# Second FFN product of an encoder step written as seven half-size block products

## The chip, the cores and the metric

The kernel runs on one core of a Trainium2 chip. The metric is the device time of one launch in microseconds (us), given as the median of the runs. The profile is of one execution and counts from the first to the last instruction of the program (its span). Engines: TensorE (PE) does matmuls and, beside them, weight loads (PEld); VectorE (DVE), ScalarE (ACT) and GpSimd (POOL) work element by element; SyncE (SP) issues nearly all DMAs.

## The reference, cut to what matters

One step of a two-layer encoder. Layer 0 is an SSD mixer and an FFN, layer 1 is band attention and an FFN. 1024 prompt frames and 64 sample frames go through the same weights, so the kernel treats them as 1088 columns.

```
D_MODEL = 1024; FFN_HIDDEN = 2816
def swiglu(u, w_in, w_out):
    g, up = jnp.split(u @ w_in, 2, axis=-1)
    return (jax.nn.silu(g) * up) @ w_out
...
x = x + post_norm(f(pre_norm(x)))      # every sub-layer, RMSNorm over D_MODEL
```

`u @ w_in` is called the first product here, `(...) @ w_out` the second. All is float32.

## The kernel before

**Layout and exactness.** Features lie on the 128 partitions, frames along the free axis. D_MODEL is 8 tiles (`KD`), the hidden width 22 tiles (`FT`). Each float32 operand is split into a rounded high part and a low rest; a product of one 128x128 weight tile takes three matmuls (high by high, high by low, low by high). The split costs one ACT cast and one DVE subtraction for weights (`Weights.part`, lines 342 and 343) and for activations alike. PE's order is the program's own order; the other engines' instructions are ordered by a scheduler with priorities. A virtual clock (`Stream`) decides where side tasks (generators with `yield`) put their instructions among the PE work.

**Frames.** Two partitions of the 1088 frames are in use: three slices `SL` of 384, 384 and 320, and four quarters `QS` of 256, 256, 288 and 288. Quarters 0 and 1 form block 0, quarters 2 and 3 block 1.

**First product.** It is already done by 2x2x2 blocks in seven products (`PRODS`: P1, P6, P2, P7, P5, P4, P3), with sums of weights made in `Weights.pair` (lines 290, 291, 308, 309) and sums of activations made once in `op_build`. `run_pair` computes one hidden tile for both blocks, 84 matmuls of 256 columns and 84 of 288, and evicts with DVE adds (lines 1328 to 1345); ACT applies silu and POOL multiplies gate by up (lines 1342, 1346). The first six hidden tiles are done in `plain_pairs` for block 0 alone, without the seven products; then 16 tiles for both blocks; then the first six for block 1. Each hidden tile is stored to DRAM (`hscr`, lines 1291, 1343, 1347).

**Second product.** In `back`, lines 1514 to 1516: for each of the three slices, for each of 8 output tiles, a sum over all 22 hidden tiles: 528 weight tiles x slice in all, three matmuls each. All weights are loaded and split once for each slice. `loader` (lines 1375 to 1377) reads hidden tiles back from DRAM, splits them and keeps a whole slice in SBUF. ACT evicts (line 1529), squares go to a running sum on POOL (line 493).

**After it.** `end` runs once for each slice: the root of the mean square (`rstd`, lines 500 to 524: PE transposes, ten small DVE operations), its broadcast (`bcast`, lines 530 and 533), scaling and residual add (lines 1430, 1431), store of x. In layer 0 it also splits the result into the operands of the attention layer (`u_slice`, `UC`: lines 1447, 1448) and makes the factor of the next norm, marked `("rb", s)`. Attention begins with K, V and Q projections of slices 0 and 1, which need `u[0]`, `u[1]`, and then the factor in their evictions; slice 2 follows. In layer 1 the last slice ends the kernel (lines 1404 to 1421).

**Buffers.** Big tiles come from two rings: `R` (16 tiles of 1152 columns) and `RX` (13 of 1024, per layer). `Ring.get` and `put` count tiles; a task waits in virtual time until a tile is free. Weights pass `raw` (2, and lent `RX` tiles) and `hl` (3 split tiles of 1024 columns).

Of the kernel before, what the change touches and what calls it, by code (L numbers as in the profile page):

```python
# [39 lines left out]
AT = mybir.DependencyInfo(mybir.DependencyClass.Sync, mybir.DependencyReason.DATA)  # L40

# [7 lines left out]
ES = 0.5, 0.5, 0.0  # L49
OS = 1.9, 1.4  # L50
EP_W, ER_W, EQ_W = (9.4, 9.4, 2.2), (8.9, 8.9, 3.3), (11.0, 11.0)
# [4 lines left out]
LDP, ENP, ATP = 1500, (0, 0, 1500), 1000  # L56
# [3 lines left out]
RAWB, HLB, SGB = 2, 3, 5  # L60
# [6 lines left out]
NACC = 3  # L67

# [155 lines left out]

class Weights:
# [44 lines left out]
    def plain(self, it):  # L270
        if not self.room():
            return False
        r, n = it["raw"][0], it.get("n", 1024)
        if it.get("kscale") is not None:
            self.scaled(it, r)
        else:
            self.part(it, "w", None, r[:, :n])
        it["of"][0].put()
        self.ready.append(self.sq.pop(0))
        return True  # L280
# [44 lines left out]
    def part(self, it, key, ring, v, eng=None, acc=None):  # L325
        if ring is not self.half:
            ring = self.hl if ring or self.hl.free() else self.hx
            self.used.append(ring)
# [50 lines left out]
def hybrid_kernel(  # L379
# [42 lines left out]
    hd_ = [dr.tile([P, FT, T], F32, name=f"hscr{i}") for i in range(2)]  # L422
# [9 lines left out]
    W.tc, W.lent = tc, Lent(RX)  # L432
    W.raws.append(W.lent)
    UC = Cells(384, (R, 99))

# [821 lines left out]

    def ffn_plan(layer):
        w1, w2 = w_f1[layer], w_f2[layer]
        W.plan(*[dict(src=[w1[i]], acc=t_ < NACC or t_ == NB0 - 1) for t_ in range(NB0) for i in (t_, FT + t_)])  # L1260
        for t_ in [*range(NB0, FT), *range(NB0)]:
            W.plan(dict(src=[w1[t_], w1[FT + t_]], pacc=t_ in (NB0, NB0 + 1)))
        for s in range(NSL):
            for m in range(KD):
                for k0, nk in KCH:
                    W.plan(dict(src=[w2[m][:, k0 * P:(k0 + nk) * P]], n=nk * P))

    KCH = ((0, 8), (8, 8), (16, 6))

    def plain_pairs(ts, ops, hd, px, tmp):  # L1270

        n = ops.n
        first = ts == PGS[0]
        xs, ws = {}, {}
        for t_, i, q in [(t_, i, q) for t_ in ts for i, q in (((0, 0), (1, 0), (0, 1), (1, 1)) if first else ((0, 0), (0, 1), (1, 0), (1, 1)))]:
# [4 lines left out]
            if i == 0:  # L1280
                xs[t_, q] = tmp.tile([P, n], F32, tag=("p1", "u3")[q] + f"{t_ % 2}", name="x")
# [6 lines left out]
            def mult(ps):  # L1288
                with tc.high_priority(HIP):
                    V.tensor_tensor(x, ps[:, :n], x, op=ALU.mult)  # L1290
                nc.sync.dma_start(hd[:, t_, q * n:(q + 1) * n], x)
# [5 lines left out]
    def run_pair(t_, pr, bs, ends, ops, hd, px, tmp, apart=False):  # L1297
# [3 lines left out]
        for (p_, key, c0, i), b in [(x, b) for b in bs for x in PRODS] if apart else [(x, b) for x in PRODS for b in bs]:  # L1301
# [3 lines left out]
            def t_new(tag):  # L1305
                return tmp.tile([P, n], F32, tag=f"{tag}{b if len(bs) > 1 else t_ % 2}", name=tag)
# [4 lines left out]
            for k in range(4):  # L1311
# [3 lines left out]
                PE.matmul(ps, wl, ah[:, k, :], start=False, stop=(k == 3))  # L1315
# [6 lines left out]
            with tc.high_priority(HIP):  # L1322
# [16 lines left out]
                elif p_ == P4:  # L1339
# [3 lines left out]
                    nc.sync.dma_start(hd[:, t_, BO[b] + n:BO[b] + 2 * n], x["u3"])  # L1343
                else:
                    V.tensor_tensor(x["u2"], ps, x["u2"], op=ALU.add)
                    G.tensor_tensor(x["c22"], x["p1"], x["u2"], op=ALU.mult)
                    nc.sync.dma_start(hd[:, t_, BO[b]:BO[b] + n], x["c22"])
# [6 lines left out]
    def back(layer, start, cpost, xsrc, xmid, cpre, cpost2, xout, rb_out, done2):  # L1354

        hd = hd_[layer]
        dn, ops, phase, hid = [], [Ops(0, layer), Ops(1, layer)], [0], [{}, {}, {}]
        with ExitStack() as es:
            px = pool(es, f"px{layer}", 4, space=PSUM)
            RX.pool, RX.bufs = pool(es, f"rx{layer}"), NRX  # L1360
            sgp = pool(es, f"sg{layer}")
            stage[0] = lambda: sgp.tile([P, 384], F32, tag="sg", bufs=SGB, name="sg")

            def loader():

                for s, (o, n) in enumerate(SL):
                    yield 0, 0, lambda: phase[0] > (s > 0)
                    cells = Cells(n, *(((RX, 99), (R, 8)), ((R, 9), (RX, 99)), ((RX, 99), (R, 3)))[s])
                    for k in range(FT):
                        yield 0, 0, lambda: cells.room(2)  # L1370
                        c = cells.get(), cells.get()
                        h_, l_ = rr(c[0][0]), rr(c[1][0])
                        t_ = stage[0]()[:, :n]
                        with tc.high_priority(LDP):
                            nc.sync.dma_start(t_, hd[:, k, o:o + n])
                            A.copy(h_, t_)
                            V.tensor_tensor(l_, t_, h_, op=ALU.subtract)
                        hid[s][k] = h_, l_, c, cells

            def end_load(s):  # L1380
                o, n = SL[s]
                xc = Cells(n, (R, 99)) if s == 2 else Cells(n, (RX, 99), (R, 99))
                yield 0, EP_W[s] if s < 2 else 0, lambda: xc.room(KD)
                xs = [xc.get() for _ in range(KD)]
                for m in range(KD):
                    nc.sync.dma_start(xs[m][0], xmid[:, m, o:o + n])
                xss[s] = xs, xc

            def end(s, y, ss, more=None):

                o, n = SL[s]
                if s not in xss:
                    yield from end_load(s)
                xs, xc = xss.pop(s)
                out = []
                if s == 2 and more is None:
                    yield 0, EP_W[2]
                steps = rb_steps(ss, n, out, ER_W[s], more=more)
                if more is not None:

                    xps = {}

                    def hold(ms):
                        for m in ms:
                            xps[m] = mm("xp") if m > 3 else px.tile([P, 512], F32, tag="mm", name="xp")
                            PE.matmul(xps[m][:, :n], ident, xs[m][0], start=True, stop=False)
# [6 lines left out]
                    for m in range(KD):  # L1413
                        ym = y[:, m, :n]
# [4 lines left out]
                        else:  # L1419
                            V.tensor_tensor(ym, ym, xs[m][0], op=ALU.add)  # L1420
                        nc.sync.dma_start(xout[:, m, o:o + n], ym)
                    for c in xs:
                        xc.put(c)
# [637 lines left out]
```

## Time and profile before

| | us |
|---|---|
| median of 3 runs | 2940.78 |
| lowest, highest | 2934.37, 2947.84 |
| profiled execution: span | 2929.9 |
| second product, layer 0 | 264.8 (from 1315.6 to 1580.4) |
| second product, layer 1 | 262.7 (from 2653.8 to 2916.5) |
| first product by pairs, layer 0 | 398.6 (from 917.0 to 1315.6) |

The profiled execution lies 10.9 us below the median of the runs and 4.5 us below the lowest of them, so a time worked out on the span is moved by the first of these to stand beside the median. Within the page: part 1 gives the busy time of each engine; matmuls overlap there, so their mean duration is not the distance from one to the next. That distance has to be read from starts in the timeline.

### The profile page before, as it was taken

The numbers are of one execution on the slowest core, as the hardware profiler recorded it, in microseconds if no ns is written. First come the engines' busy times: TensorE is split into PE (matmuls) and PEld (weight loads), VectorE is DVE, ScalarE is ACT, GpSimd is POOL, SyncE is SP. The second block draws the span as 40 slices with busy tenths as digits, with TensorE's granted clock in tenths as the row PEclk, the third lists the DMA queues.
The fourth block names the chain that finished last, engine by engine and source line by source line (L and its number), as shares of the span: only waits on it lengthen the run. The fifth ranks groups of instructions, "written<-read, shape, count | busy, mean of one in ns | idle before, by whom it ended". The sixth has DMA issues, their size and how long they took to land.

```text
span 2929.9 us, 56271 instructions
## 1 busy us (share of the span) xinstructions
PE 2897.3 (99%) x21562; PEld 2858.7 (98%) x21562; DVE 2027.6 (69%) x4452; ACT 1403.6 (48%) x2535; POOL 718.9 (25%) x884
## 2 busy tenths in 40 slices
PE   8999999999999999999999999999999999999999
PEld 8999999999999999999999899999999999999998
DVE  7988878885867555583567887778688554575544
ACT  6655546454544222353445665556664222244443
POOL 1333333331022434350111000000131434351111
PEclk9999999999999999999999999999999999999999
DMA  4423333335564222345664322223476222245654
GB/s 138 133 92 106 104 98 109 100 117 165 165 187 137 76 81 77 108 151 163 207 192 154 98 74 72 65 69 108 132 204 179 83 77 81 75 154 178 225 171 135
DMA packets 203422, 369.12 MB, mean 126 GB/s; under 512 B 20752, under 2 KB 149488, under 8 KB 203152
## 3 DMA queue, kind: packets, MB, share of 16 engines
q1 hardware_dynamic: 199920, 354.97, 38.3%
q0 software_dynamic: 3232, 10.56, 2.0%
q8 instruction: 169, 2.77, 0.4%
q14 instruction: 101, 0.83, 0.1%
HBM read 298.24 MB, written 62.74 MB: 123 GB/s over the span
## 4 chain that ended last, share of the span: by engine, by line
PE 88%; DVE 6%; DMA 2%; ACT 2%; issue 1%; SPq 0%; POOL 0%; DVEq 0%; ACTq 0%; POOLq 0%
PE px L1314 9%; PE px L1315 9%; PE px L1313 9%; PE mm L467 8%; PE mm L469 8%; PE mm L468 8%; PE po L1515 6%; PE po L1516 6%; PE po L1514 6%; PE mmx L468 3%; PE mmx L469 3%; PE mmx L467 3%; PE ptp L1747 2%; PE po L1782 2%; PE S L1716 1%
## 5 line engine op out<-in xcount | busy, mean ns | idle before, releaser
L467 PE MATMUL mm<-r,hl 128*128 128x384 f32 (+2 forms) x1704 | 566.6, 333 | 2.6 <-DVE vt L1679 1.0
L469 PE MATMUL mm<-r,hl 128*128 128x384 f32 (+2 forms) x1704 | 549.6, 323 | 1.0 <-DVE hl L343 0.7
L468 PE MATMUL mm<-r,hl 128*128 128x384 f32 (+2 forms) x1704 | 549.3, 322 | 0.0
L343 DVE TENSOR_TENSOR hl<-raw,hl 128x1024 fp32r<-128x1024 f32 x216 | 256.3, 1187 | 216.6 <-ACT hl L342 208.9
L1314 PE MATMUL px<-r,hl 128*128 128x288 f32 (+1 forms) x1184 | 347.6, 294 | 0.0
L467 PEld LDWEIGHTS mm<-r,hl 128*128 128x128 f32 x1704 | 321.9, 189 | 4.9 <-DVE vt L1679 1.3
L469 PEld LDWEIGHTS mm<-r,hl 128*128 128x128 f32 x1704 | 321.1, 188 | 1.9 <-DVE hl L343 1.0
L468 PEld LDWEIGHTS mm<-r,hl 128*128 128x128 f32 x1704 | 322.2, 189 | 0.3
L1315 PE MATMUL px<-r,hl 128*128 128x288 f32 x1056 | 311.5, 295 | 0.0
L1313 PE MATMUL px<-r,hl 128*128 128x288 f32 x1056 | 310.4, 294 | 0.0
L342 ACT CAST hl<-raw 128x1024 fp32r<-128x1024 f32 x216 | 216.8, 1004 | 162.5 <-PE po L1516 101.6
L493 POOL TENSOR_TENSOR ssum<-ssum,sq 128x256 f32<-128x256 f32 (+3 forms) x97 | 125.5, 1295 | 616.9 <-ACT sq L492 601.3
L1314 PEld LDWEIGHTS px<-r,hl 128*128 128x128 f32 x1184 | 222.4, 188 | 0.0
L1315 PE MATMUL px<-rx,hl 128*128 128x256 f32 x768 | 214.2, 279 | 3.6 <-DVE hl L343 3.5
L1313 PE MATMUL px<-rx,hl 128*128 128x256 f32 x768 | 213.9, 278 | 0.4 <-DVE x L1290 0.4
L1515 PE MATMUL po<-rx,hl 128*128 128x384 f32 (+1 forms) x624 | 202.0, 324 | 0.2
L1313 PEld LDWEIGHTS px<-r,hl 128*128 128x128 f32 x1056 | 198.9, 188 | 0.1
L1315 PEld LDWEIGHTS px<-r,hl 128*128 128x128 f32 x1056 | 198.9, 188 | 0.0
L1514 PE MATMUL po<-rx,hl 128*128 128x384 f32 (+1 forms) x608 | 197.7, 325 | 0.0
L1516 PE MATMUL po<-rx,hl 128*128 128x384 f32 (+1 forms) x608 | 196.7, 324 | 0.0
L1314 PE MATMUL px<-rx,hl 128*128 128x256 f32 x640 | 178.4, 279 | 0.0
L1514 PE MATMUL po<-r,hl 128*128 128x384 f32 (+1 forms) x448 | 148.4, 331 | 0.0
(367 smaller groups left out, 7890.1 us busy)
## 6 DMA issues: line engine op xcount, KB each, us to landing
raw<-in_w_f_dram SPq DMA_DIRECT2D x154, 512.0 KB, 3.7
rx<-in_w_f_dram SPq DMA_DIRECT2D x54, 512.0 KB, 3.7
raw<-in_w_in_dram SPq DMA_DIRECT2D x40, 512.0 KB, 3.7
MT<-ascr SPq DMA_DIRECT2D x48, 384.0 KB, 4.3
sg<-hscr SPq DMA_DIRECT2D x88, 192.0 KB, 3.4
raw<-in_w_f_dram SPq DMA_DIRECT2D x44, 384.0 KB, 3.2
raw<-in_w_so_dram SPq DMA_DIRECT2D x32, 512.0 KB, 3.7
raw<-in_w_o_dram SPq DMA_DIRECT2D x19, 512.0 KB, 3.6
```

The source lines that it names most:

```text
L342: self.nc.scalar.copy(h, v)
L343: (eng or self.eng or self.nc.vector).tensor_tensor(lo, v, h, op=ALU.subtract)
L467: PE.matmul(ps[:, :n], h_, xh, start=(first and i == 0), stop=False)
L468: PE.matmul(ps[:, :n], h_, xl, start=False, stop=False)
L469: PE.matmul(ps[:, :n], l_, xh, start=False, stop=(last and i == nk - 1))
L493: (eng or G).tensor_tensor(ssum[:, :n], ssum[:, :n], q[:, :n], op=ALU.add)
L1313: PE.matmul(ps, wh, ah[:, k, :], start=(k == 0), stop=False)
L1314: PE.matmul(ps, wh, al[:, k, :], start=False, stop=False)
L1315: PE.matmul(ps, wl, ah[:, k, :], start=False, stop=(k == 3))
L1514: PE.matmul(ps[:, :n], wh, xh, start=(k == 0), stop=False)
L1515: PE.matmul(ps[:, :n], wh, xl, start=False, stop=False)
L1516: PE.matmul(ps[:, :n], wl, xh, start=False, stop=(k == FT - 1))
```

## The change

**The second product by blocks.** The hidden axis is cut in halves (tiles 0 to 10 and 11 to 21, `KH` = 11), the output axis in halves (tiles 0 to 3 and 4 to 7), the frames of each block in its two quarters. Seven products follow, each of 4 output tiles x 11 hidden tiles x 2 blocks. Hidden tile pairs (k, k+11) are now computed one after the other, and their sums s1 to s4 are made by DVE at once (`hidden`), so that seven operands instead of the hidden tiles go to DRAM (`hc`). Four sums of the second weights are made by DVE during the first product of each layer and stored in DRAM (`w2_sums`). `loader` reads operands in groups of three or four tiles and splits them. `evict` adds up the products in place. Six products run for both blocks on one set of weights; the last, P4, runs for block 0 and then for block 1, and the weights of three of its four output tiles are kept in ring tiles (`Held`).

```
-for s, (o, n) in enumerate(SL):
-    for m in range(KD):
-        for k0, nk in KCH:            # ((0, 8), (8, 8), (16, 6))
+SEQ = tuple((p_, (0, 1)) for p_ in (P1, P6, P2, P5, P3, P7)) + ((P4, (0,)), (P4, (1,)))
+KCH, KHELD = ((0, 6), (6, 5)), ((0, 4), (4, 4), (8, 3))
+J4 = (0, 1, 2, 3), (1, 2, 3, 0)
+for x, (p_, bs) in enumerate(SEQ):
+    for j in J4[bs[-1]] if len(bs) == 1 else range(4):
+        for b in bs:
+            for c, (k0, nk) in enumerate(KHELD if keep else KCH):
+                for k in range(k0, k0 + nk):
+                    PE.matmul(ps[:, :n], wh, xh, start=(k == 0), stop=False)
+                    PE.matmul(ps[:, :n], wh, xl, start=False, stop=False)
+                    at_pe[0] = PE.matmul(ps[:, :n], wl, xh, start=False, stop=(k == KH - 1))
+            evict(p_, b, j, ps[:, :n])
```

Evictions, by DVE but for the first product (`add(t, x)` is one DVE add of the PSUM tile to x); P1 `A.copy(c11)`; P6 `add(c21, c11)`; P2 `add(c11, c11)`; P5 `add(c22, c21)`; P3 `add(c12, c22)`; P7 `add(c22, c22)` and `add(c21, c21)`; P4 `add(c21, c21)`. Quarters 0 and 2 are whole after P3, quarter 1 after P4 of block 0, quarter 3 after P4 of block 1; `ready` collects the squares and spawns `end`.

```
+def hidden(t_, b, x, z, late=None):       # x: first half of the block's frames, z: second
+    if not kh:
+        out(OPI["a11"], x)
+        out(OPI["s3"], total(s3, x, z, ALU.subtract))
+        kept[k, b] = z, s3
+        return
+    out(OPI["a12"], x)
+    out(OPI["a22"], z)
+    out(OPI["s1"], total(z0, z0, z, ALU.add))
+    s2 = total(stage[0]()[:, :n], z, s3, ALU.subtract)
+    out(OPI["s2"], s2)
+    out(OPI["s4"], total(stage[0]()[:, :n], x, s2, ALU.subtract))
...
+def w2_sums(layer, yet):                  # 16 times (4 tiles x 4 pieces of SUM_C = 352 columns)
+    paced(nc.sync.dma_start(t_, w2[m][:, a:a + SUM_C]))          # four loads
+    paced(V.tensor_tensor(b22, b22, b12, op=ALU.subtract))       # four DVE sums
+    paced(nc.sync.dma_start(wd[:, i, j, c:c + SUM_C], t_))       # four stores
...
+def loader():
+    yield 0, 0, lambda: phase[0] and stored.get((i, b)) == KH
+    yield 0, 0, lambda: any(r.free(2) for r in rings)
+    paced(nc.sync.dma_start(l_, hc[:, i, k:k + g, HO[b]:HO[b] + n]))
+def parted(p_, b, k, g, h_, l_, r):
+    paced(A.copy(rr(h_), l_))
+    paced(V.tensor_tensor(rr(l_), l_, rr(h_), op=ALU.subtract))
```

`paced` puts an instruction behind the last PE instruction in the scheduler's order and adds no wait on the chip. `hidden` stores 4.0 us (`HST`) of virtual time after the sums.

**Norms by quarter.** `end` runs for quarters. A slice of the attention operands needs two quarters: slice 0 needs 0 and 1, slice 1 needs 1 and 2, slice 2 needs 2 and 3; the same holds for the factors.

```
+EP_W, ER_W, EQ_W = (6.0, 5.0, 8.0, 4.0), (6.0, 4.0, 6.0, 4.0), (12.0, 14.0, 12.0, 16.0)
+SEG = (((0, 0, 256, 0),), ((0, 256, 384, 0), (1, 0, 128, 128)), ((1, 128, 384, 0),), ((2, 32, 320, 0),))
+for s, *_ in SEG[q]:
+    yield 0, 0, lambda: s in ucells or UC.room(2 * KD)
+...
+yield (0, EQ_W[q]) if q < 3 else (0, 0, lambda: "k2" in done2)
+yield from rb_steps(tot, n, [], ER_W[q], rb_out[:, o:o + n])
```

**Start of attention.** The matmuls of V and K for slice 0 are issued before the factor of slice 0 is there, then their evictions wait for it; Q of slice 0, then V, K and Q of slice 1 follow.

```
-for s in range(2):
-    st.wait_for(lambda: s in done)
-    for w, e in ((wv, evv), (wk, evk), (wq, evq)):
-        units(w, 0, e, (s,))
+st.wait_for(lambda: 0 in done)
+for w, e in ((wv, evv), (wk, evk)):
+    passes(ps, w, lambda k: u[0][k], [(k, k) for k in range(KD)], n0, parts=4)
+st.wait_for(lambda: ("rb", 0) in done)
+for ps, e in first:
+    e(0)(0, ps)
+units(wq, 0, evq, (0,))
+st.wait_for(lambda: 1 in done)
+for w, e in ((wv, evv), (wk, evk), (wq, evq)):
+    units(w, 0, e, (1,))
```

425 lines of the change are left out of this document (288 added, 137 removed).

## The prediction

> **What bounds the kernel now.** I read the page first: who is busy, at what clock, what chain ended last.
>
> ```profile
> span 2929.9 us, 56271 instructions
> ...
> PE 2897.3 (99%) x21562; PEld 2858.7 (98%) x21562; DVE 2027.6 (69%) x4452; ACT 1403.6 (48%) x2535; POOL 718.9 (25%) x884
> ...
> PEclk9999999999999999999999999999999999999999
> ...
> PE 88%; DVE 6%; DMA 2%; ACT 2%; issue 1%; SPq 0%; POOL 0%; DVEq 0%; ACTq 0%; POOLq 0%
> ```
>
> PE is busy almost throughout, at full granted clock. A busy PE may still be waiting inside its pipeline, so next come the windows, cut where the stages of the two FFNs begin and end (columns: PE, PEld, DVE, ACT, POOL, then clock, DMA share, GB/s).
>
> ```profile
> 833.40:917.00 83.60, 83.60 (x724) 83.60 (x723) 57.64 (x111) 39.02 (x55) 16.74 (x19) 1.00 0.79 220
> 917.00:1249.00 332.00, 329.78 (x2656) 329.41 (x2655) 181.67 (x317) 103.32 (x173) 125.18 (x109) 1.00 0.28 87
> 1249.00:1315.60 66.60, 66.60 (x506) 66.60 (x506) 54.09 (x84) 33.20 (x54) 35.19 (x28) 1.00 0.48 152
> 1315.60:1580.40 264.80, 264.59 (x1610) 263.87 (x1609) 144.91 (x219) 121.33 (x197) 37.06 (x28) 1.00 0.59 185
> ...
> 2653.80:2916.50 262.70, 262.70 (x1598) 262.56 (x1597) 121.88 (x165) 103.70 (x159) 31.81 (x24) 1.00 0.57 181
> 2916.50:2929.90 13.40, 8.73 (x41) 6.02 (x39) 6.54 (x20) 3.42 (x8) 0.00 (x0) 1.00 0.29 98
> ```
>
> The second product takes 264.8 and 262.7 us, and PE is idle for 0.2 us of it. Whether each pass runs at its own pace is read from starts in the timeline: 48 passes of 384 columns, 36 of 320, then runs of twelve of 256 and of 288 in the first product.
>
> ```profile
> 1399.79 0.33 PE L1516 MATMUL po<-rx,hl 128*128 128x384 f32 x1
> ...
> 1407.99 0.34 PE L1515 MATMUL po<-r,hl 128*128 128x384 f32 x1
> ```
> ```profile
> 1559.77 0.31 PE L1514 MATMUL po<-rx,hl 128*128 128x320 f32 x1
> ...
> 1564.90 0.31 PE L1516 MATMUL po<-rx,hl 128*128 128x320 f32 x1
> ```
> ```profile
> 1100.12 0.28 PE L1313 MATMUL px<-rx,half 128*128 128x256 f32 x1
> ...
> 1101.48 0.29 PE L1313 MATMUL px<-r,half 128*128 128x288 f32 x1
> ...
> 1103.07 0.28 PE L1313 MATMUL px<-rx,hl 128*128 128x256 f32 x1
> ...
> 1104.48 0.30 PE L1313 MATMUL px<-r,hl 128*128 128x288 f32 x1
> ...
> 1106.08 0.28 PE L1313 MATMUL px<-rx,hl 128*128 128x256 f32 x1
> ```
>
> 384 columns: 8.20 us over 47 steps, 0.1745 us. 320: 5.13 over 35, 0.1466. 256: 1.36 and 1.41 us for twelve, 0.1154. 288: 1.59 and 1.60, 0.1329. With these the old second product should take 352 x 3 x 0.1745 + 176 x 3 x 0.1466 = 261.7 us; measured 262.7 to 264.8. So the stage is its passes and nothing else: the kernel is bound by the number of PE passes.
>
> **The change, part by part.** *Fewer passes.* After it each layer has 7 x 4 x 11 x 3 = 924 passes of 256 and as many of 288: 924 x (0.1154 + 0.1329) = 229.4 us, 32.3 us less than 261.7. Both layers: **-64.6 us**. The two runs of 256 lie 0.1133 and 0.1175 apart, which bounds the term to 4 us either way.
>
> The Trainium skill, page "TensorE: Matmul & The Clock Gate", section "Back-to-back issue gap", gives for a lone stream N/2.4 + 2.5 ns; my estimate from it is 162.5, 135.8, 122.5 and 109.2 ns for the four widths, 29 us a layer, and a sum 6 us higher. No row here is that fast, and 320 and 384 columns exceed it most, so the measured steps stand.
>
> *DVE* takes most of the new work; its prices:
>
> ```profile
> L343 DVE TENSOR_TENSOR hl<-raw,hl 128x1024 fp32r<-128x1024 f32 x24 | 29.4, 1224 | 41.1 <-ACT hl L342 39.2 <-DMA r<-x1d 1.7
> ...
> L343 DVE TENSOR_TENSOR hl<-raw,hl 128x768 fp32r<-128x768 f32 x22 | 21.8, 989 | 24.9 <-ACT hl L342 24.6 <-ACT sq L492 0.3
> ...
> L1431 DVE TENSOR_TENSOR y<-y,r 128x384 f32<-128x384 f32 x16 | 8.3, 548 | 0.0
> ```
> ```profile
> L1337 DVE TENSOR_TENSOR c<-px,u 128x256 f32<-128x256 f32 x16 | 6.7, 418 | 0.1
> ```
>
> First product, 917 to 1249: 64 hidden sums of 256 or 288 columns, scaled from 548 ns for 384, 25 us, and 64 weight sums of 352 columns at 0.50, 32 us. 181.7 + 57 = 239 of 332 us. Second product: weight splits fall from 48 pieces of 1024 columns and 24 of 768 (82 us) to 40832 columns (29 sets of 1408; 53 us at 989/768 ns); operand splits rise from 22 x 1088 to 77 x 544 columns, 22 us more at 1.2 ns; 56 evictions at 0.43 us, 24 us, move here from ACT. 144.9 - 29 + 22 + 24 = 162 of 230 us. DVE stays off the path as long as its queue doesn't stand still; without that cover the 57 us a layer would be on it. I take 0.
>
> *DMAs.* In 917 to 1249 the weight sums add 16 x 8 transfers of 180 KB, 23 MB, the extra operands 7 MB: 87 GB/s becomes about 177. In the second product a product loads 2.9 MB of weights and 3.1 MB of operands in 32.8 us, 181 GB/s against 185 now. The row 833 to 917 shows 220 GB/s with PE busy in 83.60 of 83.60 us. I take 0.
>
> ```profile
> 1040.84 0.32 SPq L1343 DMA_DIRECT2D hscr<-u  x1
> ```
> ```profile
> raw<-in_w_f_dram SPq DMA_DIRECT2D x44, 384.0 KB, 3.2
> ```
>
> Each issue also takes SP about 0.32 us (194 more in the first product of a layer, 62 us in 400), and SP works in order: a store that waits for its sum holds the weight loads behind it, and PE waits for those. That the stores come 4 us of planned time after the sums is what hides it.
>
> *Start of the second product.* The first operand of block 0 is complete when the 16 joint tiles are done, 66.6 us early; that of block 1 three tiles before the end. 0, at most 3 us a layer.
>
> *Kept weights.* In P4 of block 0 a piece of 512 weight columns feeds 12 passes, 1.38 us. It goes through three raw tiles, each taken for a load (at most the 3.2 us of 384 KB), a cast and a subtraction (0.6 each), so up to 1.5 us a piece; but the loads start in P7. 1 us a layer, ends 0 and 4.
>
> *Turn from FFN 0 to attention.* Now slices 0 and 1 are ready long before PE needs them. After the change both wait for quarter 1, which is whole only one P4 (block 1) before the end: 132 x 0.1329 = 17.5 us of cover. Behind it in a row:
>
> ```profile
> L493 POOL TENSOR_TENSOR ssum<-ssum,sq 128x320 f32<-128x320 f32 x6 | 12.8, 2132 | 54.8 <-ACT sq L492 54.8
> ```
> ```profile
> 1582.06 2.42 DVE L356 SCALAR_TENSOR_TENSOR hl<-raw,pcs,hl 128x128 fp32r<-128x128 f32 x7 [0.30 <-ACT hl L352]
> ...
> 1590.13 3.79 DVE L1430 SCALAR_TENSOR_TENSOR y<-y,pcs,rb 128x320 f32<-128x320 f32 x8 [0.24 <-ACT rb L533]
> ```
> ```profile
> PE nbp L530 <- DVE nr L524: 1.3, 1, 1.3
> PE ptp L1747 <- DVE mx L1726: 1.0, 1, 1.0
> PE mm L467 <- DVE vt L1679: 1.0, 1, 1.0
> ```
>
> Eviction and square 0.9 us, POOL sum up to 2.1, root and broadcast about 3.5, eight scalings 3.1 (3.79 at 320), residual 2.4, sixteen 128-column splits 5.5 (0.35 each): 17.5; the planned delays of 5 and 4 us before the two PE steps add about 4. So PE waits some 4 us; then V and K of slice 0 (48 passes, 8.4 us) end before the factor, which needs three sums and another root: 4 us more. While the factor is awaited those two results hold both PSUM tiles of the projections, so Q of slice 0 stands behind them. Of the waits in the last fence (1580 to 1650, 3.3 us) I count 1 as gone. **+7 us**. If the operand slices also wait for tiles of ring R, held by P4's operands and the kept weights, it is 18; if scheduling closes the gaps and today's waits go, -3.
>
> *Tail of layer 1* (13.4 us): the last add now precedes the square, +0.45; eight operations at 288 instead of 320, -0.3. 0.
>
> Sum: 2929.9 - 64.6 + 7 + 2 = 2874.3 on the span; the median of the runs lies 10.9 above the span, so **2885 us**.
>
> **The rivals.**
>
> *A late turn (A).* Ring tiles, SP or the norms cost more than above: 20 to 45 us over both layers, 2905 to 2926. For: all quarters feed one another, and slices 0 and 1 both hang on quarter 1. Against: only layer 0 has the turn.
>
> *The first product becomes bound by DVE's queue (B), slower.* The sums s1, s2 and s4 read what POOL has just multiplied. DVE is in order: if it stands at such a sum, the next pair's evictions stand behind it, PSUM fills, PE stops.
>
> ```profile
> L1342 POOL TENSOR_TENSOR u<-u,c 128x288 f32<-128x288 f32 x22 | 32.1, 1457 | 34.3 <-ACT u L1341 34.3
> ...
> L1342 POOL TENSOR_TENSOR u<-u,c 128x256 f32<-128x256 f32 x16 | 12.1, 757 | 26.4 <-ACT u L1341 26.4
> ```
> ```profile
> DVE tt L308 <- POOL tt L290: 9.8, 18, 0.8
> ```
>
> Four PSUM tiles cover two products of both blocks, 6 us. There are 11 x 2 x 2 = 44 such places; to pass the gain and 0.5% more (64.6 + 15), each would have to wait 6 + 1.8 us. At 8 us: 88 us lost, 2885 + 88 = 2973. Against: DVE's waits for POOL are 0.8 us at most now. For: the same multiplication takes 757 ns at 256 columns and 1457 at 288, so the two engines do slow each other, and the change adds 300 DVE sums beside POOL's work.
>
> The Trainium skill, page "SBUF — State Buffer", section "Who interferes with whom", says that a DVE instruction with two SBUF inputs and a GpSimd one that reads SBUF lock each other out for a whole instruction; all added sums are of that kind. The doubling above agrees with it and speaks for B.
>
> *It doesn't do what it says (C).* If 256 columns took as long as 288 (a weight load as floor), 1848 x 0.0175 = 32 us would go, 2917. The rows of 256 speak against it.
>
> **How the numbers follow.** Forecast 0.72 (2868 to 2905: -64.6 with its 4 either way, ends of the turn and the kept weights, 3 either way for the runs; the upper end adds the late start, 6), A 0.14, C 0.02, a mixture that ends within 0.5% (2926 to 2955) 0.06, B 0.06. 0.5%, 14.7 us, is about what a measurement can tell from no change. Faster 0.88, same 0.06, slower 0.06. The range reaches over half of A: 2868 to 2918.
>
> **What would show it.** Right: `po` passes of 256 and 288 some 0.115 and 0.133 us apart, the second product 228 to 236 us long in both layers, first product within 3 us of 398.6, PE idle of 5 to 12 us in the 30 us after FFN 0. Wrong: PE waits for DVE in the first product (B), waits for `hid` or kept weights inside the second, or a `po` step of 0.13 at 256 columns (C).

## The result and the profile after

| | us |
|---|---|
| before, median (4 runs beside the kernel after) | 2940.78 |
| after, median (4 runs) | 2962.28 |
| ratio, 95% interval | 1.0079, 1.0060 to 1.0097 |
| span of the profiled execution, before and after | 2929.9, 2962.7 |

The kernel after is 0.8% slower; 2885 was forecast. First the page of the kernel after: its span, part 1, and the granted clock of part 2.

```profile
span 2962.7 us, 58034 instructions
...
PE 2864.9 (97%) x22096; PEld 2813.5 (95%) x22096; DVE 2221.4 (75%) x4847; ACT 1367.5 (46%) x2485; POOL 714.1 (24%) x903
...
PEclk9999999999999999999998999999999999999999
```

PE is busy for 32 us less than before (2897.3), and the span is 33 us longer: PE now stands still for some 98 us of it instead of 33. Where, the windows say, cut at the stages: first product by pairs in its start (288 passes: the first joint tile, which is done block by block, and most of the second), in the other 14.3 of the 16 joint tiles ("joint" below), in the tail (the six tiles that block 1 makes alone), second product, then from FFN 0 to the first `po` of attention, second product of layer 1, end. Columns as in the prediction: us, busy PE, PEld, DVE, ACT, POOL, clock, DMA share, GB/s.

```profile
916.70:960.00 43.30, 38.41 (x291) 37.40 (x289) 30.62 (x49) 14.85 (x22) 11.95 (x10) 0.96 0.40 120
960.00:1272.10 312.10, 301.37 (x2403) 298.09 (x2402) 220.62 (x386) 83.36 (x142) 114.28 (x100) 1.00 0.51 164
1272.10:1351.60 79.50, 72.08 (x506) 70.94 (x505) 65.22 (x94) 31.90 (x46) 34.21 (x27) 0.94 0.54 168
1351.60:1587.80 236.20, 232.39 (x1869) 231.12 (x1868) 152.72 (x254) 106.68 (x179) 34.02 (x34) 1.00 0.61 195
1587.80:1669.10 81.30, 66.71 (x372) 64.07 (x370) 65.84 (x213) 44.88 (x124) 5.42 (x18) 0.90 0.30 94
2715.80:2949.80 234.00, 231.18 (x1866) 230.41 (x1864) 140.44 (x216) 94.03 (x141) 31.57 (x32) 1.00 0.59 190
2949.80:2962.70 12.90, 8.06 (x40) 5.79 (x38) 6.18 (x20) 3.25 (x8) 0.00 (x0) 1.00 0.39 132
```

The same cuts in the kernel before, where the prediction doesn't show them (its tail is the row from 1249; the pairs begin at 913.0, 4 us ahead of the 917.0 used there):

```profile
913.00:951.30 38.30, 36.08 (x291) 35.71 (x290) 26.47 (x38) 14.97 (x22) 12.05 (x10) 1.00 0.30 89
951.30:1249.00 297.70, 297.70 (x2403) 297.70 (x2402) 158.60 (x283) 91.94 (x155) 115.28 (x101) 1.00 0.27 86
1580.50:1644.80 64.30, 60.70 (x372) 58.76 (x370) 54.79 (x164) 37.65 (x97) 2.52 (x12) 1.00 0.37 113
```

The second product fell from 264.8 to 236.2 us and from 262.7 to 234.0. The first product took that back: in layer 0 +5.0 us in its start, +14.4 in the joint part, +12.9 in the tail. From the last `po` of FFN 0 to the last one of attention (the turn below) it is 524.2 before and 545.5 after, +21.3, of which 17 lie in the row 1587.80 and 4 between the first and the last `po` of attention (459.8 us before, 463 to 465 in every kernel with the change). All stages (lengths from first to last matmul): first products +32.3 and +33.2, second -28.8 and -28.9, turn +21.3, before the pairs (with the tiles that block 0 makes alone) +3.7, the rest 0; together +32.8, the difference of the spans.

What happens in a joint tile is in DVE's timeline (start, duration, line, tiles; in brackets the idle time ahead and who ended it):

```profile
1123.50 1.50 DVE L1455 TENSOR_TENSOR sg<-c,u 128x256 f32<-128x256 f32 x1 [1.88 <-POOL c L1421]
1124.92 0.44 DVE L1420 TENSOR_TENSOR u<-px,u 128x288 f32<-128x288 f32 x1
1126.34 0.46 DVE L1455 TENSOR_TENSOR sg<-c,u 128x288 f32<-128x288 f32 x1 [0.98 <-POOL c L1421]
1126.72 0.52 DVE L1333 TENSOR_TENSOR wsum<-wsum 128x352 f32<-128x352 f32 x1
1127.27 0.53 DVE L1334 TENSOR_TENSOR wsum<-wsum 128x352 f32<-128x352 f32 x1
1127.83 0.53 DVE L1335 TENSOR_TENSOR wsum<-wsum 128x352 f32<-128x352 f32 x1
1128.39 0.53 DVE L1336 TENSOR_TENSOR wsum<-wsum 128x352 f32<-128x352 f32 x1
1128.83 0.78 DVE L1404 TENSOR_TENSOR u<-px,p 128x256 f32<-128x256 f32 x2
```

DVE stands 1.88 us for POOL's product, makes the sum s3 of block 0 beside POOL in 1.50 us, evicts once, stands 0.98 us again, makes s3 of block 1, then four weight sums in a row (2.1 us). Only at 1128.83 does it evict P6 (L1404), 7.2 us after it began to wait. PE has meanwhile filled all four PSUM tiles, with P6 and P2 of both blocks (timeline of PE):

```profile
1122.61 0.28 PE L1389 MATMUL px<-rx,hl 128*128 128x256 f32 x1
...
1129.31 0.39 PE L1389 MATMUL px<-rx,hl 128*128 128x256 f32 x1 [0.58 <-DVE u L1404]
```

Filling them took from 1122.61 to 1128.73, 6.1 us; the first tile is free only some 6.6 us after 1122.61, and PE stands 0.58 us. It stops so 13 times in the joint part, its weight loads 14 times (waits in 960 to 1272; total, times, longest):

```profile
DVE sg L1455 <- POOL c L1421: 24.9, 21, 1.9
...
PEld px L1389 <- DVE u L1404: 14.0, 14, 1.5
...
DVE u L1455 <- POOL u L1418: 13.0, 15, 1.3
...
PE px L1389 <- DVE u L1404: 10.7, 13, 1.2
```

The 14.0 us of the weight loads are nearly the 14.4 that the joint part lost. There are 14 rows of four weight sums in this stretch, and each of the 14 waits ends 0.9 to 1.0 us after the last sum of such a row has begun.

DVE is busy for 220.6 of 312 us here, 71%; the forecast, 239 of 332, was 72%. It is not full; it stands still 38 us for POOL (20.0 of them ahead of s3) at places where evictions queue behind it. And the hidden sums come in two lengths (same stretch; ns min/median/max):

```profile
L1455 DVE TENSOR_TENSOR u<-u,u x15: 424/426/1542, 964.6 to 1271.4; 128x256 f32<-128x256 f32 x8, 128x288 f32<-128x288 f32 x7
L1455 DVE TENSOR_TENSOR sg<-u,sg x15: 418/421/446, 964.9 to 1271.8; 128x256 f32<-128x256 f32 x8, 128x288 f32<-128x288 f32 x7
```

The second of these two sums (s2) never takes over 0.45 us, the first (s1) up to 1.54. The Trainium skill, page "SBUF — State Buffer", section "Who interferes with whom", says that a DVE instruction with two SBUF inputs and a GpSimd one that reads SBUF exclude each other, the later one blocking until the first is done; these rows agree: a 1.5 us sum is 0.42 us of work and about one POOL operation (the s3 of 1.50 us above began 0.08 us after a POOL operation of 1.29 us, L372).

### The profile page after: what moved, and what is told of

It is laid out like the page before. It is cut to its first block, busy times and chain, and to the rows that moved or that the text cites. A ratio compares the mean times of both kernels' runs of the same rounds, so it can differ in the third digit from the quotient of the medians.

```text
span 2962.7 us, 58034 instructions
## 1 busy us (share of the span) xinstructions
PE 2864.9 (97%) x22096; PEld 2813.5 (95%) x22096; DVE 2221.4 (75%) x4847; ACT 1367.5 (46%) x2485; POOL 714.1 (24%) x903
## 5 line engine op out<-in xcount | busy, mean ns | idle before, releaser
L1389 PE MATMUL px<-r,hl 128*128 128x288 f32 x1056 | 314.9, 298 | 19.3 <-DVE u L1404 8.7
L1391 PE MATMUL px<-r,hl 128*128 128x288 f32 x1056 | 314.9, 298 | 0.0
L372 DVE TENSOR_TENSOR hl<-raw,hl 128x1024 fp32r<-128x1024 f32 (+2 forms) x188 | 208.2, 1110 | 141.4 <-ACT hl L371 141.3
L530 POOL TENSOR_TENSOR ssum<-ssum,sq 128x256 f32<-128x256 f32 (+1 forms) x111 | 123.2, 1111 | 573.2 <-ACT sq L529 553.4
L371 ACT CAST hl<-raw 128x1024 fp32r<-128x1024 f32 (+2 forms) x188 | 178.9, 951 | 124.0 <-PE po L1729 86.2
L1390 PEld LDWEIGHTS px<-r,hl 128*128 128x128 f32 x1184 | 225.9, 191 | 0.0
L1389 PEld LDWEIGHTS px<-r,hl 128*128 128x128 f32 x1056 | 201.9, 191 | 22.3 <-DVE u L1404 10.3
L1391 PEld LDWEIGHTS px<-r,hl 128*128 128x128 f32 x1056 | 202.1, 191 | 0.2 <-DVE hl L372 0.2
L1727 PE MATMUL po<-r,hl 128*128 128x288 f32 (+1 forms) x682 | 196.6, 288 | 0.0
L1728 PE MATMUL po<-r,hl 128*128 128x288 f32 (+1 forms) x682 | 196.4, 288 | 0.0
L1729 PE MATMUL po<-r,hl 128*128 128x288 f32 (+1 forms) x682 | 196.4, 288 | 0.0
L1389 PEld LDWEIGHTS px<-rx,hl 128*128 128x128 f32 x768 | 145.7, 190 | 31.6 <-DVE u L1404 29.9
```

What stands on the lines that cost most here:

```text
L371: self.nc.scalar.copy(h, v)
L372: (eng or self.eng or self.nc.vector).tensor_tensor(lo, v, h, op=ALU.subtract)
L530: (eng or G).tensor_tensor(ssum[:, :n], ssum[:, :n], q[:, :n], op=ALU.add)
L1389: PE.matmul(ps, wh, ah[:, k, :], start=(k == 0), stop=False)
L1390: PE.matmul(ps, wh, al[:, k, :], start=False, stop=False)
L1391: at_pe[0] = PE.matmul(ps, wl, ah[:, k, :], start=False, stop=(k == 3))
```

## The experiments

Theory (order): the sums cost time in the first product because of where they stand in DVE's in-order queue; the evictions behind them come late and PSUM runs out. Rivals: traffic (the added DMAs delay weights), amount (DVE has too much to do beside POOL, in whatever order), buffers (a single buffer makes ACT, POOL and DVE wait for each other). Stage lengths are of layer 0, in us, each from one profiled execution, whose time lies within some 9 us of its kernel's median; "turn" is as above. e1 to e4, e16 and e18 leave work out: they show costs and are no alternatives. Each ratio is to runs of the kernel before on the same chip.

| kernel | median | ratio (95%) | joint | tail | turn |
|---|---|---|---|---|---|
| before | 2937 to 2941 | 1 | 297.7 | 66.8 | 524.2 |
| after | 2962.28 | 1.0079 (1.0060-1.0097) | 312.1 | 79.7 | 545.5 |
| e1 | 2926.74 | 0.9957 (0.9941-0.9974) | 298.2 | 75.2 | 545.3 |
| e2 | 2925.37 | 0.9962 (0.9947-0.9977) | 298.1 | 78.0 | 544.9 |
| e3 | 2917.52 | 0.9935 (0.9916-0.9954) | 298.2 | 73.3 | 542.9 |
| e4 | 2932.73 | 0.9982 (0.9972-0.9991) | 299.0 | 79.4 | 548.3 |
| e5 | 2961.29 | 1.0072 (1.0056-1.0087) | 313.9 | 80.4 | 538.7 |
| e6 | 2944.58 | 1.0018 (1.0008-1.0028) | 303.9 | 81.6 | 543.2 |
| e7 | 2956.41 | 1.0057 (1.0036-1.0078) | 309.5 | 81.4 | 542.5 |
| e8 | 2962.01 | 1.0077 (1.0061-1.0094) | 312.7 | 79.9 | 543.2 |
| e9 | 2930.80 | 0.9978 (0.9968-0.9987) | 298.5 | 78.3 | 539.6 |
| e10 | 2936.25 | 0.9995 (0.9985-1.0004) | 298.4 | 80.1 | 540.8 |
| e11 | 2929.19 | 0.9963 (0.9949-0.9977) | 298.8 | 78.7 | 541.7 |
| e12 | 2941.06 | 1.0006 (0.9995-1.0016) | 300.9 | 78.0 | 541.9 |
| e13 | 2961.62 | 1.0076 (1.0061-1.0091) | 312.5 | 79.7 | 547.6 |
| e14 | 2933.99 | 0.9988 (0.9980-0.9997) | 298.8 | 79.5 | 540.9 |
| e15 | 2927.94 | 0.9970 (0.9959-0.9980) | 299.2 | 79.6 | 541.6 |
| e16 | 2905.80 | 0.9885 (0.9870-0.9899) | 298.2 | 69.2 | 544.8 |
| e17 | 2941.11 | 1.0007 (0.9998-1.0016) | 299.4 | 73.7 | 539.3 |
| e18 | 2926.61 | 0.9954 (0.9937-0.9970) | 298.7 | 77.0 | 538.1 |

### What the sums cost: e1 to e4

e1, weight sums left out with their loads and stores:

```
 def w2_sums(layer, yet):
+    yet.append(layer)
+    return
...
-    if p_ in W2S:
-        return wd_[layer][:, W2S[p_], j, :]
-    m, kh = {P1: (j, 0), P2: (j, 1), P3: (j + 4, 1)}[p_]
+    m, kh = {P1: (j, 0), P2: (j, 1), P3: (j + 4, 1), P6: (j + 4, 0), P7: (j, 0), P5: (j, 1), P4: (j + 4, 1)}[p_]
```

> Left out: the four sums of the second weights with their loads and stores; P6, P7, P5 and P4 take plain weight tiles instead. Theory 'queue' (DVE works in order and stands at the new sums, or does four weight sums in a row, just ahead of the first evictions of the next hidden tile; PSUM's four tiles run out, PE waits 1.1 us a tile): the 2.1 us of weight sums are more than the 1.1 us missing, so the joint part falls to its old length; the tail and the start of the stage keep their losses. First product by pairs of layer 0 from 434.5 to 405-415 us, kernel 2910-2925 us. Rival 'traffic' (the first product moves 158 GB/s instead of 87, so weights come late): falls too, by as much as traffic falls (23 of 30 MB): 2900-2915. Rival 'buffers' (fewer or other tiles for u2, u3, p1 and the new order of hidden tiles): no change, 2955-2965.

e2, hidden sums left out (`x` or `z` is stored in place of s1 to s4):

```
-out(OPI["s3"], total(s3, x, z, ALU.subtract))
+out(OPI["s3"], x)
...
-out(OPI["s1"], total(z0, z0, z, ALU.add))
+out(OPI["s1"], z)
```

> Left out: the sums s1 to s4 of the hidden tiles; x or z is stored in their place, so the transfers are the same. Queue: DVE no longer waits for POOL's product and no longer runs beside it at 1.5 us a sum; joint part and tail fall: first product by pairs of layer 0 398-406 us, kernel 2895-2905 us. Traffic: no change, 2955-2965. Buffers: no change.

e3, both edits:

> Left out: both kinds of sums, with the transfers of the weight sums. Queue: not much beyond the run without hidden sums, since either removal alone clears the joint part: 2885-2900 us. Traffic: as the run without weight sums. Buffers: 2955-2965.

e4, only DVE's four operations of the weight sums left out:

```
-paced(V.tensor_tensor(b22, b22, b12, op=ALU.subtract))
-paced(V.tensor_tensor(b12, b12, b11, op=ALU.subtract))
-paced(V.tensor_tensor(b11, b22, b11, op=ALU.add))
-paced(V.tensor_tensor(b21, b21, b11, op=ALU.subtract))
```

> Left out: only the DVE operations of the weight sums; loads and stores stay, so the weight tiles in DRAM are unsummed. Queue: as the run without weight sums at all, within 8 us (2910-2930). Traffic: as the changed kernel, 2955-2965. This run alone separates the two.

Either kind of sum, taken out alone, brings the joint part wholly back to 298 us; taking out both gives no more. This is no sum of two costs but a threshold: the queue's delay exceeds PSUM's 6 us only when both stand in it. Traffic falls as the main cause: in e4 every load and store is still there, and 29.5 of e1's 35.5 us come back (by the ratios, 0.97 of 1.22%). Buffers fall for the joint part: e1 to e3 keep the single ones. e1 and e4 came out 2 and 3 us above what I had expected of the theory, e2 20 and e3 17, since I had looked for the whole loss in the sums: tail and turn stay long without any.

### Order or amount in the joint part: e6, e7, e9

e6, the four weight sums apart:

```
 paced(V.tensor_tensor(b22, b22, b12, op=ALU.subtract))
+yield 0, SUM_GAP / 12
 paced(V.tensor_tensor(b12, b12, b11, op=ALU.subtract))
+yield 0, SUM_GAP / 12
...
```

> The four weight sums of a piece are issued 1.5 us apart instead of one after the other; their number, size, loads and stores are as in the kernel after. Theory order (four sums of 0.52 us stand in a row between evictions on DVE's queue, and with the sums that wait for POOL they use up the four PSUM tiles): the joint part falls from 312 to 298-303 us in each layer, the first product from 435 to 421-427 us, the time to 2936-2950 us. Rival amount (DVE has too much to do beside POOL, whatever the order): joint part 308-314 us, time 2954-2966 us.

e7, the hidden sums of a pair later (`HDL` 3.0, and `later` yields 1.0 after each; `f2` makes s2, and s3 is spawned in the same way):

```
-out(OPI["s1"], total(z0, z0, z, ALU.add))
-s2 = total(stage[0]()[:, :n], z, s3, ALU.subtract)
...
+st.spawn(later(
+    lambda: out(OPI["s1"], total(z0, z0, z, ALU.add)), f2,
+    lambda: out(OPI["s4"], total(stage[0]()[:, :n], x, s2[0], ALU.subtract)),
+), HDL)
```

> The four hidden sums of a pair of tiles are issued 3 us later and 1 us apart, so that DVE does not stand waiting for POOL's product; number and size are as in the kernel after. Theory order: the joint part falls from 312 to 298-304 us in each layer, the time to 2936-2952 us. Rival amount: joint part 308-314 us, time 2954-2966 us. If only the row of weight sums counted (it stands here as before), the joint part would keep more than 306 us here and lose it in e6_weight_sums_spread.

e9, both, and the edit of e5 (below):

> The edits of e5_last_block_order, e6_weight_sums_spread and e7_hidden_sums_later together; everything is computed as in the kernel after. Theory order: with the row of weight sums broken up and no sum standing behind POOL, the joint part comes to 297-301 us in each layer, as with the sums left out (298), the first product to 418-425 us, the turn to last po to 533-540 us, the time to 2915-2932 us. Rival amount: what the two edits give adds up at most (8 and 3-4 us of the joint part), the joint part stays at 301-308 us and the time at 2930-2945 us.

e6 brings back 8 of the 14 us (303.9, just above the 303 expected), e7 3 (in the rival's range: with the weight sums in a row it isn't enough), both all of it. Neither number nor size of any operation has changed. The windows of e9's joint part and tail, and DVE's waits for POOL in the joint part:

```profile
958.40:1256.90 298.50, 298.40 (x2403) 298.16 (x2402) 233.75 (x383) 85.76 (x142) 113.97 (x100) 1.00 0.53 172
1256.90:1335.10 78.20, 70.82 (x507) 69.88 (x506) 66.14 (x95) 32.50 (x47) 36.02 (x28) 0.96 0.55 170
```
```profile
DVE u L1459 <- POOL u L1422: 9.1, 7, 1.3
...
DVE sg L1459 <- POOL c L1425: 3.7, 14, 0.3
```

DVE is busy for longer than in the kernel after (233.8 against 220.6 us, since more sums run beside POOL), in a shorter stretch, and PE waits for nothing: for the joint part amount falls, order stands. The weight sums show how little a lock matters by itself (groups of L1336, first after, then e9, of 960 to 1272 and 958 to 1257):

```profile
L1336 DVE TENSOR_TENSOR wsum<-wsum 128x352 f32<-128x352 f32 x14 | 7.4, 525 | 0.5
```
```profile
L1336 DVE TENSOR_TENSOR wsum<-wsum 128x352 f32<-128x352 f32 x14 | 11.4, 817 | 0.0
```

### The tail: e8, e11, e13, e14, e16, e17

e8, DVE's subtraction of an operand piece apart from ACT's copy:

```
 paced(A.copy(rr(h_), l_))
+yield 0, 3.0
 paced(V.tensor_tensor(rr(l_), l_, rr(h_), op=ALU.subtract))
```

> Of each operand piece of the second product, ACT's copy is issued as before and DVE's subtraction 3 us later. Theory in-order (in the tail of the first product, 79.7 us against 66.8 before, DVE stands before evictions because its subtraction waits for ACT's copy of up to 1152 columns): tail 70-76 us in each layer, time 2945-2956 us. Rival length (the two subtractions of 1.7 us each stand before the evictions whether or not they wait): tail 77-81 us, time 2957-2966 us. The joint part stays at 312 us by both.

e11 is e9, e13 the kernel after, each with two buffers in the tail:

```
-return tmp.tile([P, n], F32, tag=f"{tag}{b}", bufs=2 if tag == "u3" or (tag == "p1" and not b) else 1, name=tag)
+s = T_TAIL.index(t_) % 2 if len(bs) == 1 and tag != "u3" else b
+m = 288 if tag != "u3" else n
+return tmp.tile([P, m], F32, tag=f"{tag}{s}", bufs=2 if tag == "u3" or (tag == "p1" and not s) else 1, name=tag)[:, :n]
```

> As e9_three_edits, and in the six tiles that block 1 makes alone, p1, u2 and c22 alternate between the buffers of block 0 and those of block 1, as the kernel before does, where the kernel after keeps one of each. Theory buffers (ACT's copy of P1 waits until POOL has read the one p1 and its product c, which puts the 16.0 us of DVE's idle at L1404 into e3_no_sums' tail, and PE stands 2 us a tile for it): the tail falls from 78.3 to 70-74 us in each layer, the time by 8-16 us to 2915-2924 us. Rival amount (DVE is busy 66 of the tail's 78 us and only its amount of work counts): tail 76-80 us, time within 4 us of e9_three_edits.

> The kernel after with the buffers of p1, u2 and c22 alternating in the tail and nothing else changed. Theory buffers: tail from 79.7 to 71-76 us in each layer, joint part still 312 us, time 2946-2955 us. Rival amount: tail 77-81 us, time 2957-2966 us.

e14, e11 with the tail's sums later (`HDT` 5.5) and the operand splits in pieces:

```
-), HDL)
+), HDT if b and k < NB0 // 2 else HDL)
...
-paced(V.tensor_tensor(rr(l_), l_, rr(h_), op=ALU.subtract))
 for x in range(g):
+    paced(V.tensor_tensor(rr(l_[:, x, :]), l_[:, x, :], rr(h_[:, x, :]), op=ALU.subtract))
```

> As e11_tail_buffers, with three of the hidden sums of the tail's tiles issued 5.5 us instead of 3 us after the pair, behind the evictions of P6 and P2, and DVE's subtraction of an operand piece cut into one for each 256 or 288 columns, 1 us apart in the tail. Theory order (in the tail too PE waits because sums and subtractions of 1.3 to 3.4 us stand ahead of an eviction): tail from 78 to 71-75 us in each layer, the time to 2915-2925 us. Rival amount (DVE is busy 66 of 78 us and beside POOL each operation takes three times as long): tail 76-80 us, time 2926-2934 us.

All four leave the tail at 77 to 80 us in both layers: waits for ACT, single buffers and order, each alone, are not its limit while the sums are there. What is left is seen where the sums are gone. In e3's tail (groups, then waits):

```profile
L1404 DVE TENSOR_TENSOR u<-px,p 128x288 f32<-128x288 f32 x6 | 2.7, 458 | 16.0 <-ACT p L1401 16.0
```
```profile
ACT p L1401 <- POOL c L1421: 20.1, 6, 4.6
```

DVE is idle for 16.0 us, once a tile, for ACT's copy of P1, and that waits until POOL has read the only buffer of `p1`. The kernel before alternates two in the tail. So there should be two limits, one behind the other. e16 is e3 with e11's buffers:

> e3_no_sums (all eight sums, and the loads and stores of the weight sums, left out) with p1, u2 and c22 alternating between two buffers in the tail. Theory two limits (in the tail either limit alone gives some 6 us: without sums the single buffers, in whose wait DVE stood idle for 16 us; with sums the amount of DVE's work, so that e11 gained nothing): tail from 73.3 to 66-70 us in each layer, time 2902-2913 us. Rival (something else that the new tail has, its DMAs or its weights): tail 72-75 us, time within 4 us of e3_no_sums.

e17 is e11 with the operands of the second product begun later:

```
 if t_ == T_BOTH[-1]:
     phase[0] = 1
     W.lent.cap = 2
-    st.spawn(loader())
+if t_ == T_TAIL[-1]:
+    st.spawn(loader())
```

> As e11_tail_buffers, but the loading and splitting of the second product's operands begins only at the tail's last pair. Theory amount (the tail is long because DVE has 66 us of work in it; without the operands' 9 us of splits it has 57): tail from 78 to 69-73 us in each layer; what is won is lost again at the start of the second product, which waits for its operands, so the time stays within 10 us of e11_tail_buffers. Rival (the hidden sums alone set the tail): tail 76-80 us.

The tails in windows: e3, e16, e11, e17.

```profile
1256.30:1329.50 73.20, 67.73 (x507) 66.83 (x506) 48.97 (x71) 32.16 (x46) 32.38 (x27) 1.00 0.56 181
```
```profile
1254.30:1323.50 69.20, 67.28 (x507) 66.81 (x507) 52.50 (x74) 32.11 (x47) 34.72 (x28) 1.00 0.59 188
```
```profile
1256.60:1335.20 78.60, 71.04 (x506) 69.87 (x505) 67.53 (x96) 32.96 (x49) 35.87 (x28) 0.96 0.54 170
```
```profile
1257.50:1331.30 73.80, 68.17 (x506) 66.78 (x505) 59.45 (x91) 28.22 (x43) 34.98 (x29) 1.00 0.45 140
```

Without sums, the buffers give 4.1 us (73.3 to 69.2; 5.3 in layer 1), as expected, and the time was never lower. With the sums they give nothing in layer 0 (e11, e13) and 1 to 2 us in layer 1: something else hides them there. Amount could be that: DVE is busy for 67.5 of 78.6 us, and 8 us less of that (e17) make the tail 5 us shorter, to just above the 69 to 73 expected. But it is not shown. e17 also takes away a part of ACT's copies and of the traffic (140 GB/s instead of 170), and DVE's busy time does not order the tails: e2 has less of it than e1 (55.7 against 61.1 us) and the longer tail (78.0 against 75.2). e17 loses its gain again: PE stands 4 us between the tail and the second product, which then takes 245.4 us instead of e11's 237.8. It ends 12 us above e11, where I had allowed 10.

### The turn: e5, e10, e12, e15, e18

PE's waits from 1587.8 to 1669.1 in the kernel after, and in the same stretch of e5:

```profile
PE nbp L567 <- DVE nr L561: 5.9, 1, 5.9
PE mm L506 <- DVE hl L385: 3.4, 1, 3.4
PE nst L537 <- POOL ssum L530: 2.1, 1, 2.1
```
```profile
PE nbp L567 <- DVE nr L561: 5.8, 1, 5.8
PE nst L537 <- POOL ssum L530: 1.8, 1, 1.8
PE nst L537 <- DVE ssum L1590: 1.4, 1, 1.4
```

e5: `J4 = (0, 1, 2, 3), (0, 1, 2, 3)` instead of `(0, 1, 2, 3), (1, 2, 3, 0)`.

> The last joint product P4 of block 1 takes its output tiles in the order 0, 1, 2, 3 instead of 1, 2, 3, 0, in both layers; so the tile whose weights lie in the common ring comes first and the ring is free for the weights of attention 14 us earlier. Theory weights (the 3.4 us idle at 1595.7 us, in which PE waited for the scaled weights of K, and the half clock after it, come from that ring): the turn from the last po of FFN 0 to the last po of attention falls from 545.5 to 533-539 us and the time to 2950-2957 us. Rival norms (PE would only wait the longer for the root of the last quarters, DVE L561): turn within 3 us of 545.5, time 2959-2966 us. The first products stay at 435 us by both.

The 3.4 us for attention's weights are gone and the turn is 6.8 us shorter: P4's last tile had held ring `hl` (some 5 us, if the scatter below is taken in). The median fell by 1 us only and the span by 3.1, not by the 5 or more expected: the first product of layer 0 and both second products came out 1 to 3 us longer, for which I have no cause.

e10 is e9 with `ER_W[3]` 7.0 instead of 4.0 and `EQ_W[1]` 8.0 instead of 14.0:

> As e9_three_edits, and the root of quarter 1 is issued 6 us sooner, with 3 us more between the two halves of the roots of quarter 3, so that PE has matmuls ahead of the broadcast that waits for the root. Theory norms (the 5.9 us before nbp and the half clock behind it come from where the roots stand in PE's and DVE's queues): the turn to last po falls a further 5-12 us below that of e9_three_edits, the time likewise. Rival chain (the root comes when DVE's work of the last two quarters is done, wherever it is issued): turn within 3 us of e9_three_edits.

e12 is e11 with quarter 1's sum over tiles on PE:

```
+for i in range(nb):
+    for m, t in enumerate(sq):
+        PE.matmul(sp[:, i:i + 1], t[:, i * P:(i + 1) * P], ones[:, 0:1], start=(m == 0), stop=(m == len(sq) - 1))
...
+if sq is None:
+    V.tensor_tensor(y[0], y[0], y[1], op=ALU.add)
...
```

> As e11_tail_buffers, and the sum over the tiles of y for the second norm of quarter 1 is made by 16 matmuls of one column on PE instead of three additions and a reduction of together 2.9 us on DVE, with the root issued 6 us sooner. Theory amount in the turn (DVE has work without a gap from 1583 to 1620 us in the kernel after, so the root comes as much sooner as DVE has less to do ahead of it): the turn to last po falls 3-8 us below that of e11_tail_buffers, the time likewise. Rival order (the root's small operations stand between the big ones of quarter 3 in any case): within 2 us.

e15 is e11 with quarter 3 behind quarter 1's root (and `EQ_W[1]` 6.0):

```
+if q == 3 and rb_out is not None:
+    yield 0, 0, lambda: 1 in roots
```

> As e11_tail_buffers, but at the end of FFN 0 quarter 3 is scaled only once the second root of quarter 1 has been issued, and that root 8 us sooner. Theory order in the turn (the root's eight small operations, 0.15 us each, take 5 us because the scaling of quarter 3 stands between them): the turn to last po falls from 541.7 to 530-538 us, the time by as much to 2917-2926 us. Rival amount (what is moved behind the root is late for attention's third slice instead): turn within 3 us of 541.7 or above it.

e18 is e11 with less work for DVE:

```
-V.tensor_tensor(y[h], y[h], xs[h], op=ALU.add)
+if rb_out is None:
+    V.tensor_tensor(y[h], y[h], xs[h], op=ALU.add)
...
-V.tensor_tensor(y[0], y[0], y[1], op=ALU.add)
-V.tensor_tensor(y[0][:, 0:2, :], y[0][:, 0:2, :], y[0][:, 2:4, :], op=ALU.add)
```

> As e11_tail_buffers, but at the end of FFN 0 the residual is not added, and the second norm sums two of the eight tiles: 4 additions of 1.2-1.35 us and 4 of 0.7-1.3 us fewer on DVE for quarters 1 and 3 together, 9 us of some 33. Theory amount in the turn: the turn to last po falls from 541.7 to 531-537 us. Rival chain (PE waits on the length of a chain of small steps across engines, not on DVE's amount): turn 539-543 us.

Where the root is issued (e10), what PE takes over (e12) and what stands between its small operations (e15) leave the turn at 541 to 542 us: PE's waits change places there and don't go. e10 was 5 us slower than e9, and e12 even 12 us slower than e11, part of it in the joint tiles; that I did not follow up. Nine us less of DVE's work (e18) gave 3.6 against e11, below the forecast of 5 to 11 and above the rival's.

How far one such length can be trusted, the table shows. Ten kernels that leave the turn as in the kernel after have 542.5 to 548.3 us, 544.8 in the mean. The five that change nothing there but `J4` (e5, e9, e11, e14, e17) have 538.7 to 541.7, 540.0 in the mean. So the held ring is worth some 5 us. e18 lies 2 us below the second mean, which is within the scatter, and PE still waits 5.6 us for the root there (5.8 in e11): that DVE's amount counts is not shown. Of 21 us, then, some 5 are the held ring and 4 lie inside attention; the other 12 stay open. That they lie in the length of the chain from quarter 1's last eviction to its second root is argued and not shown. The half clock behind the waits (0.90 in the row 1587.80, 8 us of PE's work by my estimate of 0.10 x 81.3) is a part of each of these shares.

## Why the prediction was wrong

- **Fewer passes, -64.6.** Right in mechanism: -57.7 with the start of the product and the kept weights, for which I had added 2. Both second products, 236.2 and 234.0 us, lie at the upper end of the 228 to 236 forecast. PE stands 3.8 and 2.8 us there, 3.0 and 2.2 of them for weights of P4 that were not split yet (L371, L372); 1 us a layer was in the sum for that. Rival C is out: twelve steps of 256 columns in the second product take 1.36 us, 0.1133 each (timeline of PE in the kernel after).

```profile
1351.73 0.28 PE L1728 MATMUL po<-rx,hl 128*128 128x256 f32 x1
...
1353.09 0.28 PE L1728 MATMUL po<-rx,hl 128*128 128x256 f32 x1
```

- **DVE in the first product, 0: the step that failed.** "DVE stays off the path as long as its queue doesn't stand still ... I take 0." It stood still. Measured: +65.5 us in the two layers, 28.6 in the joint part, 25.4 in the tail, 11.4 in the start. 49 of them are gone without the sums (e3), and 27 of these are the joint part, won back by order alone (e9). How the sums lengthen the tail is open, and no run was aimed at the start, which keeps some 5 us a layer in e9. My rival B had the mechanism, but I priced it as one wait of 6 + 1.8 us at each of 44 places and so gave it 0.06. It left out s3, which reads POOL's product too and has the longest waits, and the weight sums. DVE's waits are of 1 to 1.9 us; but weight sums and locked sums (those slowed beside POOL) stand in the same row, and it is the row that must end before PE has filled the four PSUM tiles: 6.6 us against 6.1 at 1122.61. The share of 71%, which I had computed rightly, says nothing of that.
- **Not in the sum at all: the tail's buffers.** The change took the second buffers of `p1`, `u2` and `c22` out of the tail. Worth 4.1 and 5.3 us in the two layers once the sums are away; I had read over it.
- **DMAs, 0.** Nearly right: 164 GB/s in the joint part, and e4 against e1 leaves 6 us for the weight sums' traffic in both layers.
- **Turn, +7.** Measured +21.3, beyond the end of 18 that I had given for tiles held too long. That end's mechanism was there, in ring `hl` instead of R (some 5 us); 12 us stay open.
- **Tail of layer 1, 0.** Right (13.4 to 12.9 us). **Span to median, +10.9:** the median after is 0.4 below its span; the distance belonged to one execution before. **Range:** the ends named for it, added end to end, give 2866 to 2915 us and not 2868 to 2905; 2962 lies outside of both.

On the span: 65.5 + 4.9 (second products) + 14.3 (turn) + 3.7 (before the first product) = 88.4 us, the distance from 2874.3 to 2962.7.

A version that beats both exists: e9 and e11 compute the same and take 0.2 to 0.4% less than the kernel before (e15, 0.3%), 1.1% less than the kernel after. That is less than the 0.5% that I had called measurable, though the intervals exclude 1, and far from the 1.9% forecast.

## What to carry to other kernels

When work is added to an engine that evicts PSUM, don't ask for its share of busy time: add up the longest row of waits and operations that can stand ahead of one eviction, with sums beside POOL at the length that they have there (1.5 us here, not 0.42), and compare it with the time in which PE fills its PSUM tiles. In the joint part either kind of sum alone (e1, e2), or both spread apart (e9), cost 1 us a layer at most; both in one row cost 14. And compare the buffer counts of every temporary on both sides of a diff, because a second limit can hide behind the first.

## What the runs showed of the hardware

PE's clock can halve in a wait of 2.4 us; with the waits of up to 1.2 us in the joint part it stayed at 1.00. In the kernel after, PE's timeline at 1593 (384 columns), and at 1333 (288):

```profile
1593.97 0.34 PE L504 MATMUL mm<-r,hl 128*128 128x384 f32 x1
...
1595.73 0.34 PE L505 MATMUL mm<-r,hl 128*128 128x384 f32 x1
1599.50 0.69 PE L506 MATMUL mm<-r,hl 128*128 128x384 f32 x1 [3.43 <-DVE hl L385]
1599.99 0.52 PE L504 MATMUL mm<-r,hl 128*128 128x384 f32 x1
...
1602.23 0.52 PE L505 MATMUL mm<-r,hl 128*128 128x384 f32 x1
```
```profile
1333.13 0.29 PE L1391 MATMUL px<-r,hl 128*128 128x288 f32 x1
1335.85 0.61 PE L1389 MATMUL px<-r,hl 128*128 128x288 f32 x1 [2.43 <-DVE u L1404]
1336.25 0.44 PE L1390 MATMUL px<-r,hl 128*128 128x288 f32 x1
...
1338.41 0.44 PE L1390 MATMUL px<-r,hl 128*128 128x288 f32 x1
```

Ahead of the wait ten passes of 384 columns take 1.76 us, 0.176 each; behind it seven take 2.24 us, 0.32 each. At 1333 the wait is 2.43 us, and passes of 288 columns then lie 0.24 us apart instead of 0.133. The granted clock within the first wait (windows; the clock is the third figure from the end):

```profile
1596.10:1598.30 2.20, 0.00 (x0) 0.00 (x0) 2.20 (x10) 1.79 (x7) 0.00 (x0) 1.00 0.00 0
1598.30:1599.50 1.20, 0.00 (x0) 0.00 (x0) 1.20 (x9) 0.00 (x0) 0.00 (x0) 0.51 0.00 0
```

The Trainium skill, page "TensorE: Matmul & The Clock Gate", section "What's actually happening", puts the gate at half clock after at least one idle window of some 3.4 us. Neither case agrees: in the first the clock falls 2.2 us after the last pass has ended, and the second wait is shorter than such a window. So a wait can cost more than its length: the mean granted clock fell from 0.998 to 0.991 of the span, which by my estimate is 0.007 x 2960 = 21 us of PE's work, against 98 - 33 = 65 us of added waiting.
